# Expert 0's rows by one-hot matmuls from token rows split in SBUF, and its tables spread over its products

## The chip, the cores and the metric

The kernel runs on one core of one Trainium2 chip. The metric is the device time of one execution in microseconds (us). The kernel before takes 1868.66, the median of three runs (1867.42 to 1868.82). Engine names: PE is TensorE, DVE is VectorE, ACT is ScalarE, POOL is GpSimd, SP is SyncE (here it issues most transfers).

## What is computed

One encoder layer on 1024 tokens of 1024 numbers: windowed attention and multi-scale pooling, gated and mixed, an out-projection with LayerNorm, then a mixture of 32 experts with 4 per token, and a second LayerNorm.

```
mixed = g_attn * a_br + g_pool * p_br
h = layer_norm(DEEPNORM_ALPHA * h + mixed @ w_out, ln1_g, ln1_b)
logits = h @ w_router + b_router
top_vals, top_idx = lax.top_k(logits, 4);  gates = softmax(top_vals)
for each expert e, on the rows xb that chose it:
    u = xb @ w_mlp1[e] + b_mlp1[e]
    gate = minimum(u[:, :1024], 7);  up = clip(u[:, 1024:], -7, 7)
    y = ((up + 1) * gate * sigmoid(1.702 * gate)) @ w_mlp2[e] + b_mlp2[e]
h = layer_norm(DEEPNORM_ALPHA * h + sum over a token's experts of gates * y, ln2_g, ln2_b)
```

## The kernel before

All large products run as three matmuls of 16-bit parts: an f32 operand is split into hi (f16) and lo (bf16, what hi leaves), and hi*hi, lo*hi and hi*lo are summed in PSUM. Every engine executes its instructions in the order in which the program writes them; nothing reorders them, so an instruction that waits holds up all that stands behind it on its engine. Tiles are handed over by semaphores.

**The dense stage** (`dense`) ends with the out-projection: a loop over 8 tiles t of 128 tokens. The mixed branches lie transposed and split in `mth` and `mtl` (written in `branch`, L555 and L556). One iteration makes two column halves c: 24 matmuls into a PSUM tile `pb`, L602 adds the residual into `z`, and LayerNorm takes statistics (L57); after both halves `rstd` and `apply` (L74, L75 for each half) finish z, the new h of the tile. Between these steps the loop weaves the router of the tile before (`Router`, called `hooks`): 8 transposes of z (L673), ACT's `hh` (L681) and DVE's `hl` (L682) make the split transposed rows, 24 small matmuls the logits (L696 to L698), `topk`, `pos_mm` and `place` give each token its place in its experts' lists and write the one-hot rows `oh` of expert 0 (L974), `gates` the softmax (ACT's `e`, L748), `tables` a transposed table `P4T` (L768). `hooks.step(t - 1)` at the top of iterations 1 to 6 prefetches one half of expert 0's weights: ACT's `wh` (L943) and DVE's `wl` (L948), 128x2048 each. z is written in f32 to `hD` in DRAM.

**The expert stage** (`experts`, `main`) takes the 32 experts r in order of load, with capacities from 176 down to 109 rows. An expert is 6 products: four column blocks of W1, (1, r, 0) to (1, r, 3), and two of W2, of 96 matmuls each (L1088 to L1090); the list `seq` interleaves the W2 products of expert r - 1 with the W1 products of r. Product i prepares the weights of product i + 2 (3 buffers): `wh` half 0, `wl` half 0, `wh` half 1, and `wl` half 1 at its end. Around the products hang tables of steps: `start`, `mid` (after the first of a product's groups, 48 matmuls), `end`.

For a later expert the chain is: `onehot(r)` on DVE (8 instructions, from the ranks table `spr`), `slot_mm(r)` (16 matmuls, L1003, from `cols`), `gather(r)` (DVE's `ig`, then POOL's indirect DMA of f32 rows of `hD`, L1019), `x_tr` (8 f32 transposes per tile, L1053), `x_hi` (ACT's `xh`, L1064) and `x_lo` (DVE's `xl`, L1069). For expert 0 this runs at the start of `main`, before product 0. `ranks` sorts the experts by load (`key` to `eb`), reads the order and the biases (`eid`, `b1r`, `b2r`), makes `spr` and `cols` from `P4T` (L834, L836), and an overflow table (30 small DVE instructions, L841 to L872); all of it behind `cum4` stands in the middle of product 0, and gather(1) at its end. After the last W1 product of an expert ACT makes `ah` (L1137) and DVE `al` (L1148), which the W2 products read; in DVE's order a `wl` stands ahead of `al`.

## Time and profile before

| | us |
|---|---|
| median of 3 runs | 1868.66 (1867.42 to 1868.82) |
| profiled execution, its own time | 1867.19 |
| its span in the trace | 1865.3 |
| dense stage up to the last logits | 572.6 |
| product 0 begins | 595.3 |
| product 3 begins | 631.6 |
| TensorE / DVE / ACT busy, share of the span | 94% / 83% / 65% |
| granted TensorE clock, mean (1 is 2.4 GHz) | 0.979 |

The span runs from the first to the last instruction that the trace holds. A share of busy time is a mean over stages with different limits, so the stages have to be read apart. Idle time of an engine that is not the bottleneck costs nothing.

### The profile page before, as it was taken

What the parts mean: (1) busy time and instruction counts of PE and PEld (TensorE: products, weight loads), DVE (VectorE), ACT (ScalarE), POOL (GpSimd) and SP (SyncE); (2) the same over time, 40 slices, a digit from 0 to 9 for tenths busy, and PEclk for the clock granted to TensorE, in tenths of its full rate; (3) what the DMA queues carried; (4) which work ended last, traced back from release to release, by engine and by line L of the source; (5) the groups of instructions that cost most, each with busy time, mean ns of one, the idle gap of its engine ahead of it and who ended that gap; (6) DMA issues with size and microseconds to landing.
All of it is one profiled execution on the core that took longest, in us unless ns stands there. A gap on an engine that the chain in (4) does not pass through costs nothing.

```text
span 1865.3 us, 53770 instructions
## 1 busy us (share of the span) xinstructions
PE 1759.6 (94%) x23150; PEld 1496.6 (80%) x23150; DVE 1555.0 (83%) x2248; ACT 1221.7 (65%) x1679; POOL 555.6 (30%) x586
## 2 busy tenths in 40 slices
PE   7998999999896999999999999999999999999980
PEld 6455554444444999999999999999999999999980
DVE  4587863234696999999999999999999999999985
ACT  4455632223121588888778888888888888888873
POOL 1336420000012523354333343234332432342111
PEclk9999999999997999999999999999999999999995
DMA  5100032112554699999999999999999999999965
GB/s 181 52 24 24 24 100 67 46 46 100 208 209 180 215 330 363 367 359 352 338 349 358 359 356 367 358 373 363 370 366 376 375 362 373 374 372 365 366 231 200
DMA packets 245955, 494.20 MB, mean 265 GB/s; under 512 B 10982, under 2 KB 32870, under 8 KB 245712
## 3 DMA queue, kind: packets, MB, share of 16 engines
q1 hardware_dynamic: 234432, 453.03, 67.3%
q0 software_dynamic: 10992, 36.62, 8.0%
q8 instruction: 184, 3.01, 0.7%
q10 hardware_dynamic: 288, 1.05, 0.1%
q14 instruction: 59, 0.48, 0.1%
HBM read 458.34 MB, written 32.33 MB: 263 GB/s over the span
## 4 chain that ended last, share of the span: by engine, by line
PE 76%; DVE 13%; ACT 4%; issue 3%; DMA 2%; POOL 0%; SPq 0%; POOLq 0%; DVEq 0%; ACTq 0%
PE mm L1088 18%; PE mm L1090 18%; PE mm L1089 18%; PE mm L108 4%; PE mm L107 4%; PE mm L109 4%; DVE wl L948 3%; PE tr L1157 2%; PE tr L1053 2%; PE pb L109 2%; PE pb L107 2%; PE pb L108 2%; ACT wh L943 1%; DVE s L344 1%; DVE ms L346 1%
## 5 line engine op out<-in xcount | busy, mean ns | idle before, releaser
L948 DVE SCALAR_TENSOR_TENSOR wl<-raw,wh 128x2048 bf16<-128x2048 f32 x384 | 874.0, 2285 | 23.4 <-ACT wh L943 22.9
L1090 PE MATMUL mm<-xh,wl 128*128 128x123 f16 (+30 forms) x4096 | 743.9, 223 | 1.9 <-DVE wl L948 1.8
L1088 PE MATMUL mm<-xh,wh 128*128 128x123 f16 (+30 forms) x4096 | 744.2, 223 | 0.6 <-ACT xh L1064 0.6
L1089 PE MATMUL mm<-xl,wh 128*128 128x123 bf16 (+30 forms) x4096 | 743.9, 223 | 0.3 <-DVE nv L745 0.3
L943 ACT ACTIVATE wh<-raw 128x2048 f16<-128x2048 f32 x384 | 725.9, 1910 | 11.4 <-PE mm L1089 8.8
L1090 PEld LDWEIGHTS <-wl 128*128 128x128 bf16 x6144 | 598.1, 97 | 5.7 <-DVE wl L948 2.7
L1089 PEld LDWEIGHTS <-wh 128*128 128x128 f16 x6144 | 598.7, 97 | 3.6 <-issue 2.8
L1088 PEld LDWEIGHTS <-wh 128*128 128x128 f16 x6144 | 596.6, 97 | 0.9
L1088 PE MATMUL mm<-ah,wh 128*128 128x123 f16 (+30 forms) x2048 | 372.6, 223 | 2.1 <-ACT ah L1137 2.1
L1089 PE MATMUL mm<-al,wh 128*128 128x123 bf16 (+30 forms) x2048 | 372.4, 223 | 1.9 <-DVE al L1148 1.9
L1090 PE MATMUL mm<-ah,wl 128*128 128x123 f16 (+30 forms) x2048 | 372.4, 223 | 0.0
L1019 POOL DMA_INDIRECT x<-hD,ig x51 | 71.8, 1408 | 563.9 <-DVE st L1008 298.9
L1169 POOL DMA_INDIRECT accD<-y,is x51 | 109.0, 2137 | 226.8 <-ACT yT L1112 96.4
L107 PE MATMUL mm<-xth,wh 128*128 128x512 f16 x400 | 151.7, 379 | 1.2 <-DVE ypl L102 1.1
L109 PE MATMUL mm<-xth,wl 128*128 128x512 f16 x400 | 151.6, 379 | 0.0
L108 PE MATMUL mm<-xtl,wh 128*128 128x512 bf16 x400 | 151.6, 379 | 0.0
L1165 ACT ACTIVATE y<-tr,gt 128x512 f32<-128x512 f32 (+11 forms) x102 | 65.3, 682 | 59.9 <-PE tr L1157 31.1
L109 PEld LDWEIGHTS <-wl 128*128 128x128 bf16 x528 | 51.7, 98 | 62.3
L108 PEld LDWEIGHTS <-wh 128*128 128x128 f16 x528 | 51.7, 98 | 56.8 <-issue 1.3
L1132 ACT ACTIVATE th<-pre 128x492 f32<-128x492 f32 (+30 forms) x64 | 42.3, 661 | 81.9 <-DVE pre L1120 81.9
L107 PEld LDWEIGHTS <-wh 128*128 128x128 f16 x528 | 51.7, 98 | 55.0 <-DVE kk L211 0.2
L161 DVE SCALAR_TENSOR_TENSOR wl<-raw,wh 128x768 bf16<-128x768 f32 (+1 forms) x30 | 24.3, 865 | 81.9 <-ACT wh L157 81.7
(305 smaller groups left out, 2545.5 us busy)
## 6 DMA issues: line engine op xcount, KB each, us to landing
raw<-in_w_mlp_dram SPq DMA_DIRECT2D x384, 1024.0 KB, 12.0
raw<-in_w_in_dram SPq DMA_DIRECT2D x13, 1024.0 KB, 5.2
...
```

What stands on the lines that cost most here:

```text
L107: nc.tensor.matmul(ps, wh(k), xh(k), start=first and i == 0, stop=False)
L108: nc.tensor.matmul(ps, wh(k), xl(k), start=False, stop=False)
L109: nc.tensor.matmul(ps, wl(k), xh(k), start=False, stop=last and i == n - 1)
L943: nc.scalar.activation(WT[i][0][:, a:b], RAW[i, h], AF.Copy, scale=WS)
L948: nc.vector.scalar_tensor_tensor(lo[:, a:b], RAW[i, h], WS, hi[:, a:b], op0=OP.mult, op1=OP.subtract)
L1019: nc.gpsimd.indirect_dma_start(out=x[:n], out_offset=None, in_=hD, in_offset=IO(ap=ig[:n, c], axis=0))
L1088: nc.tensor.matmul(ps[:, j], wh[:, k, fs], h[:, k, :Cr], start=k == 0, stop=False)
L1089: nc.tensor.matmul(ps[:, j], wh[:, k, fs], l[:, k, :Cr], start=False, stop=False)
L1090: nc.tensor.matmul(ps[:, j], wl[:, k, fs], h[:, k, :Cr], start=False, stop=k == KT - 1)
L1132: nc.scalar.activation(th[:, :, :Cr], v, AF.Tanh, scale=0.5 * 1.702 / WS)
L1165: nc.scalar.activation(E[r]["ys"][j][:n, c * 512:(c + 1) * 512], E[r]["yp"][j][:n].rearrange("p a b -> p (a b)"), AF.Copy, scale=E[r]["gt" ...
L1169: nc.gpsimd.indirect_dma_start(out=accD, out_offset=IO(ap=E[r]["is_"][:n, j:j + 1], axis=0), in_=E[r]["ys"][j][:n], in_offset=None, comput ...
```

## The change

`mth` and `mtl` get a layout by token tile, and once the out-projection has used a tile's part, z of that tile is kept there, split: `row_hi`, two ACT copies behind LayerNorm's halves (L684), and `row_lo`, one DVE subtraction of 128x1024 (L688) behind `hl`. `hD` holds the two 16-bit parts of a row side by side instead of f32. Expert 0's x is not gathered: 128 matmuls of 128x176 (`x0_mm`) multiply the rows by the one-hot rows, as far as rows and one-hots are there, and `x0_out` splits the result. Of `ranks`, the order of the experts and the biases now stand in the middle of product 0, the overflow table at its end, `spr` and `cols` in the middle of product 1, slots of expert 0 and `onehot(1)` at the end of product 1, gather(1) in the middle of product 2, its transposes in the middle of product 3. Later experts transpose the 16-bit parts: 16 transposes per tile, and a copy each on ACT and DVE. In the last three products `ah` and `al` stand ahead of the next weights' split.

```diff
-    mth = mp.tile([P, KT, S], F16, name="mth")
-    mtl = mp.tile([P, KT, S], BF16, name="mtl")
+    mth = mp.tile([P, NT, KT, P], F16, name="mth")
+    mtl = mp.tile([P, NT, KT, P], BF16, name="mtl")
...
-                mm3(ps, lambda k: mth[:, k, tk], lambda k: mtl[:, k, tk],
+                mm3(ps, lambda k: mth[:, t, k], lambda k: mtl[:, t, k],
...
-        hooks.pos_mm(t - 1) if t == NT - 1 else None
+        if t == NT - 1:
+            hooks.x0_mm(range(3), range(6))
+            hooks.pos_mm(t - 1)
+            hooks.x0_mm(range(3, 4), range(6))
         for h in range(2):
             ln.apply(z, g1, b1, z, slice(h * 512, (h + 1) * 512))
+            hooks.row_hi(t, h)
             if t == NT - 1:
                 hooks.tr_mm(t, h)
+                hooks.x0_mm(range(4 + h, 5 + h), range(6))
         hooks.write(t, z)
     hooks.place(NT - 2)
     for h in range(2):
         hooks.tr_out(NT - 1, h)
+    hooks.row_lo(NT - 1)
     hooks.logits(NT - 1)
     hooks.topk(NT - 1)
+    hooks.x0_mm(range(4), range(6, KT))
     hooks.pos_mm(NT - 1)
     hooks.place(NT - 1)
+    hooks.gates(NT - 2)
+    hooks.x0_mm(range(4, 7), range(6, KT))
+    hooks.x0_mm(range(6, 7), range(6))
+    hooks.x0_mm(range(7, 8), range(KT))
+    hooks.x0_out()
...
-        nc = self.nc
-        q = nc.scalar if t == NT - 1 else nc.sync
-        q.dma_start(self.hD[t * P:(t + 1) * P, :], z)
+        q = self.nc.scalar if t == NT - 1 else self.nc.sync
         q.dma_start(self.accD[t * P:(t + 1) * P, :], z)
+
+    def row_hi(self, t, h):
+
+        s = slice(h * 4, h * 4 + 4)
+        z = self.z[t][:, h * 512:(h + 1) * 512].rearrange("p (k q) -> p k q", q=P)
+        self.nc.scalar.activation(self.rows[0][:, t, s], z, AF.Copy)
+
+    def row_lo(self, t):
+        nc, (hi, lo) = self.nc, self.rows
+        nc.vector.tensor_sub(lo[:, t], self.z[t].rearrange("p (k q) -> p k q", q=P), hi[:, t])
+        tk = slice(t * P, (t + 1) * P)
+        nc.sync.dma_start(self.hD[tk, :D], hi[:, t].rearrange("p k q -> p (k q)"))
+        nc.sync.dma_start(self.hD[tk, D:], lo[:, t].bitcast(F16).rearrange("p k q -> p (k q)"))
+
+    def x0_mm(self, tiles, ks):
+
+        nc, c = self.nc, self.moe.c0
+        for k2 in range(ks[0] // 2, (ks[-1] + 2) // 2):
+            if k2 not in self.px:
+                ps = self.pb.tile([P, 512], F32, name="pb") if k2 < 3 else self.pt.tile([P, 4, P], F32, name="tp")
+                self.px[k2] = (ps if k2 < 3 else ps.rearrange("p a b -> p (a b)"))[:, :2 * c].rearrange("p (k c) -> p k c", c=c)
+            for k in (2 * k2, 2 * k2 + 1):
+                for t in tiles:
+                    for j in range(2):
+                        nc.tensor.matmul(self.px[k2][:, k % 2], self.rows[j][:, t, k], self.moe.oh0(t),
+                                         start=t == 0 and j == 0 and k % 2 == 0, stop=t == NT - 1 and j == 1 and k % 2 == 1,
+                                         skip_group_check=True)
+
+    def x0_out(self):
+        for k2 in range(4):
+            self.moe.x0_put(k2, self.px.pop(k2))
...
+        self.row_lo(t)
...
+    def x0_put(k2, ps):
+        s = slice(2 * k2, 2 * k2 + 2)
+        nc.scalar.activation(E[0]["xh"][:, s, :caps[0]], ps, AF.Copy)
+        nc.vector.tensor_sub(E[0]["xl"][:, s, :caps[0]], ps, E[0]["xh"][:, s, :caps[0]])
+
+    def oh0(t):
+        return E[0]["oh"][:, t, :caps[0]]
...
         def gather(r):
-                x = wk1.tile([P, D], F32, name=f"x{i}")
+                x = wk1.tile([P, 2 * D], F16, name=f"x{i}")
                 nc.gpsimd.indirect_dma_start(out=x[:n], out_offset=None, in_=hD, in_offset=IO(ap=ig[:n, c], axis=0))
                 xs.append(x)
-            rows(r, 0, 5 if r else 2)
+            E[r].update(xs=xs, xh=None)
+            targets(r)
...
+            i, s0, n, lo = part
+            dt, ident = ((F16, C["ident16"]), (BF16, C["identb"]))[lo]
+            tp = pt.tile([P, KT, n + n % 2], dt, name="tr")[:, :, :n]
+            for k in range(KT):
+                row = E[r]["xs"][i][:n, lo * D + k * P:lo * D + (k + 1) * P]
+                nc.tensor.transpose(tp[:, k], row.bitcast(BF16) if lo else row, ident[:n, :n])
...
-        slot_mm(0, 0, 2)
-        gather(0)
+        router.gates(NT - 1)
         rctx = ExitStack()
         rsb = rctx.enter_context(tc.tile_pool(name="r_sb", bufs=1, reuse_waits="tile"))
         rk = ranks(tc, C, R, rsb, lambda shape, dt: pm.tile(shape, dt, name="mm"))
         next(rk)
-        refill()
-        for part in xparts(0):
-            x_tr(0, part)
-            x_hi(0, part)
-            x_lo(0, part)
-        router.gates(NT - 2)
-        router.gates(NT - 1)
-
-        def tables():
+
+        def order():
             next(rk)
-            slot_mm(0, 2, 5)
-            rows(0, 2, 5)
-            gates(0)
-            onehot(1)
-            for _ in rk:
-                pass
-
-        def first_rows():
-            slot_mm(1)
-            gather(1)
+            refill()
+
+        def late():
+            next(rk)
             rctx.close()
             LATE["b"] = ctx.enter_context(tc.tile_pool(name="e_lb", bufs=2, reuse_waits="tile"))
             LATE["a"] = ctx.enter_context(tc.tile_pool(name="e_la", bufs=1, reuse_waits="tile"))
@@ -1208,20 +1251,32 @@
             for y in LATE["y"][0] + LATE["y"][1]:
                 nc.gpsimd.memset(y, 0.0)
 
-        at(mid, 0, tables)
-        at(end, 0, first_rows)
+        def slots0():
+            slot_mm(0)
+            targets(0)
+            onehot(1)
+
+        at(mid, 0, order)
+        at(end, 0, late)
+        at(mid, 1, next, rk)
+        at(end, 1, slots0)
+        at(mid, 2, slot_mm, 1)
+        at(mid, 2, gather, 1)
         for r in range(1, NR):
             b = first[r]
             if r > 1:
-                at(start, max(b - 9, 0), onehot, r)
-                at(end, max(b - 8, 0), slot_mm, r)
-                at(start, max(b - 7, 1), gather, r)
+                at(start, max(b - 9, 3), onehot, r)
+                at(end, max(b - 8, 3), slot_mm, r)
+                at(start, max(b - 7, 4), gather, r)
             parts = xparts(r)
             for j, part in enumerate(parts):
-                s_ = max(b - 1 - len(parts) + j, 1)
-                at(end, s_, x_tr, r, part)
-                at(x_evac, s_ + 1, x_hi, r, part)
-                at(x_evac, s_ + 1, x_lo, r, part)
+                if r == 1:
+                    at(mid, 3, x_tr, r, part)
+                    at(end, 3, x_out, r, part)
+                else:
+                    s_ = b - 1 - len(parts) + j
+                    at(end, s_, x_tr, r, part)
+                    at(x_evac, s_ + 1, x_out, r, part)
...
+            product = 0 < i <= NS and seq[i - 1][0] == 1
+            if product and i >= NS - 3:
+                post_a(i - 1)
+                post_p(i - 1)
+                product = False
             if split:
                 w_hi(n, 0)
-            if 0 < i <= NS and seq[i - 1][0] == 1:
+            if product:
                 post_a(i - 1)
             if split:
                 w_lo(n, 0)
                 refill()
                 w_hi(n, 1)
-            if 0 < i <= NS and seq[i - 1][0] == 1:
+            if product:
                 post_p(i - 1)
```

ACT in the out-projection loop, before: one iteration with its neighbours (`e` belongs to the gates, `hh` to the router's split rows).

```order
286 L943 ACTIVATE wh<-raw 128x2048
287 L748 ACTIVATE e_5337,den<-vm,nv 128x4
288 L681 ACTIVATE hh<-tp 128x512 x2
289 L768 ACTIVATE P4T<-tp 128x128
290 L943 ACTIVATE wh<-raw 128x2048
291 L748 ACTIVATE e_5496,den<-vm,nv 128x4
```

And now:

```order
288 L811 ACTIVATE P4T<-tp 128x128
289 L684 ACTIVATE mth<-z 128x512 x2
290 L989 ACTIVATE wh<-raw 128x2048
291 L791 ACTIVATE e_5357,den<-vm,nv 128x4
292 L723 ACTIVATE hh<-tp 128x512 x2
293 L811 ACTIVATE P4T<-tp 128x128
294 L684 ACTIVATE mth<-z 128x512 x2
295 L989 ACTIVATE wh<-raw 128x2048
```

The two copies `mth<-z` (they read the finished z) have come in directly ahead of `wh`, which stood behind `P4T`.

DVE at the end of one iteration and the start of the next, before:

```order
571 L74 SCALAR_TENSOR_TENSOR z<-z,ln_mv_4986,g_3409 128x512
572 L75 SCALAR_TENSOR_TENSOR z<-z,ln_r_4987,b_3410 128x512
573 L74 SCALAR_TENSOR_TENSOR z<-z,ln_mv_4986,g_3409 128x512
574 L75 SCALAR_TENSOR_TENSOR z<-z,ln_r_4987,b_3410 128x512
575 L948 SCALAR_TENSOR_TENSOR wl<-raw,wh 128x2048
576 L602 SCALAR_TENSOR_TENSOR z<-pb,xt_4847 128x512
577 L57 BN_STATS ln_st_5141<-z 128x6
```

and in the middle of it, before and now:

```order
555 L753 TENSOR_TENSOR eq<-eq,e_5024 128x128
556 L755 TENSOR_REDUCE G<-eq 128x32
557 L682 TENSOR_TENSOR hl<-tp,hh 128x512 x2
558 L602 SCALAR_TENSOR_TENSOR z<-pb,xt_4775 128x512
559 L57 BN_STATS ln_st_4985<-z 128x6
```

```order
557 L796 TENSOR_TENSOR eq<-eq,e_5036 128x128
558 L798 TENSOR_REDUCE G<-eq 128x32
559 L724 TENSOR_TENSOR hl<-tp,hh 128x512 x2
560 L688 TENSOR_TENSOR mtl<-z,mth 128x1024
561 L603 SCALAR_TENSOR_TENSOR z<-pb,xt_4782 128x512
562 L57 BN_STATS ln_st_4997<-z 128x6
```

`mtl<-z,mth` has come in behind `hl`; the piece around `wl`, from `L74` to `ln_st`, stands as before, so `wl` is still the next instruction behind the last `L75`.

DVE at the end of the ranks' work and the start of the later experts', before (`tabs` is the last of the overflow table, `ig` and `st` are expert 1's, `pre` and `th` the activation):

```order
802 L872 COPY tabs<-tab 128x128
803 L1107 TENSOR_TENSOR pre<-mm,b1r 128x2x176
804 L1017 CAST ig<-sl 128x1
805 L1017 CAST ig<-sl 10x1
806 L1008 COPY st<-sl 128x5
807 L1008 COPY st<-sl 10x5
808 L1038 SCALAR_TENSOR_TENSOR st<-st 128x1
809 L1039 SCALAR_TENSOR_TENSOR st<-st 128x1
810 L1038 SCALAR_TENSOR_TENSOR st<-st 10x1
811 L1039 SCALAR_TENSOR_TENSOR st<-st 10x1
812 L1107 TENSOR_TENSOR pre<-mm,b1r 128x2x176
813 L1120 TENSOR_SCALAR pre<-pre 128x4x176
```

And now, the piece that ends with expert 1's `ig` (`st` in the first rows is expert 0's, `oh` expert 1's one-hot):

```order
807 L1088 COPY st<-sl 128x5
808 L1088 COPY st<-sl 48x5
809 L1102 SCALAR_TENSOR_TENSOR st<-st 128x1
810 L1103 SCALAR_TENSOR_TENSOR st<-st 128x1
811 L1102 SCALAR_TENSOR_TENSOR st<-st 48x1
812 L1103 SCALAR_TENSOR_TENSOR st<-st 48x1
813 L1063 TENSOR_SCALAR oh<-iotaC,spr 128x138 x8
814 L1180 TENSOR_SCALAR pre<-pre 128x4x176
815 L1181 SCALAR_TENSOR_TENSOR pre<-pre,th 128x4x176
816 L994 SCALAR_TENSOR_TENSOR wl<-raw,wh 128x2048
817 L1205 TENSOR_TENSOR al<-pre,ah 128x4x176
818 L1077 CAST ig<-sl 128x1
```

`ig` stood behind `tabs` and one `pre`, ahead of product 3's `wl`; now both halves of product 3's `wl`, the tables `spr` and `cols`, the one-hots and the first half of product 4's `wl` stand ahead of it.

## Rows read from the trace of the kernel before

**Rows 1.** The page's first part: busy time of each engine, its share of the span and its instructions.

```profile
PE 1759.6 (94%) x23150; PEld 1496.6 (80%) x23150; DVE 1555.0 (83%) x2248; ACT 1221.7 (65%) x1679; POOL 555.6 (30%) x586
```

**Rows 2.** The table by stretches: the stretch and its length, busy time (and number of instructions) of PE, PEld, DVE, ACT and POOL, then TensorE's granted clock, the DMA share and GB/s; a stretch of the out-projection loop, one of the passage to the experts, one of the products.

```profile
500.00:520.00 20.00, 17.47 (x131) 9.28 (x129) 18.32 (x45) 4.52 (x9) 3.96 (x16) 1.00 0.68 239
580.00:600.00 20.00, 13.25 (x168) 11.61 (x167) 10.88 (x43) 3.55 (x9) 5.61 (x20) 0.50 0.67 239
660.00:760.00 100.00, 100.00 (x1620) 99.06 (x1618) 95.00 (x123) 83.30 (x100) 32.78 (x31) 1.00 1.00 349
```

**Rows 3.** DVE's timeline over one iteration of the out-projection loop: start, duration, engine, line, operation, tiles and shapes, and in brackets the idle time before it with its releaser.

```profile
512.48 2.28 DVE L948 SCALAR_TENSOR_TENSOR wl<-raw,wh 128x2048 bf16<-128x2048 f32 x1
...
517.12 0.16 DVE L751 RECIPROCAL den<-den 128x1 f32<-128x1 f32 x1 [0.46 <-ACT e L748]
...
525.45 0.75 DVE L75 SCALAR_TENSOR_TENSOR z<-z,ln_r,b 128x512 f32<-128x512 f32 x1
526.12 2.28 DVE L948 SCALAR_TENSOR_TENSOR wl<-raw,wh 128x2048 bf16<-128x2048 f32 x1
```

**Rows 4.** ACT's timeline in the same iteration.

```profile
520.05 0.28 ACT L768 ACTIVATE P4T<-tp 128x128 f16<-128x128 f16 x1 [1.99 <-PE tp L767]
520.23 1.90 ACT L943 ACTIVATE wh<-raw 128x2048 f16<-128x2048 f32 x1
```

**Rows 5.** The waits from 500 to 570: the waiting engine and operation, its releaser, us in total, times, longest.

```profile
PE mm L698 <- DVE hl L682: 5.5, 5, 1.1
```

**Rows 6.** Groups of instructions by line and shape: count, busy us and mean ns of one, then the idle time before them. ACT's copy into `mth` in the branches, DVE's `hl` in the loop, and an operation of 128x1024 in f32 in the last LayerNorm.

```profile
L555 ACT ACTIVATE mth<-t 128x512 f16<-128x512 f32 x3 | 1.9, 629 | 9.5 <-DVE t L554 9.5
L682 DVE TENSOR_TENSOR hl<-tp,hh 128x512 bf16<-128x512 f32 x10 | 6.4, 678 | 0.0
L1508 DVE SCALAR_TENSOR_TENSOR a<-a,sums,g 128x1024 f32<-128x1024 f32 x8 | 10.0, 1278 | 0.0
```

**Rows 7.** DVE's timeline behind the loop, as far as expert 1's `ig`.

```profile
572.24 0.69 DVE L602 SCALAR_TENSOR_TENSOR z<-pb,xt 128x512 f32<-128x512 f32 x1 [0.40 <-PE pb L109]
...
582.48 0.19 DVE L706 SCALAR_TENSOR_TENSOR lg<-mm,br 128x32 f32<-128x32 f32 x1 [0.55 <-PE mm L698]
...
613.76 0.20 DVE L1017 CAST ig<-sl 128x1 int32<-128x1 f32 x2
```

**Rows 8.** TensorE's timeline behind the loop, as far as product 3.

```profile
575.70 0.18 PE L726 MATMUL mm<-mask,upper 128*128 128x32 f16 x1 [2.84 <-DVE mask L718]
577.75 1.08 PE L673 MATMUL tp<-identf,z 128*128 128x128 f32 x4 [1.85 <-DVE z L75]
...
591.73 2.98 PE L1053 MATMUL tr<-identf,x 128*128 128x128 f32 x16 [0.82 <-DMA x<-hD,ig]
595.30 0.31 PE L1088 MATMUL mm<-xh,wh 128*128 128x176 f16 x1 [0.58 <-ACT xh L1064]
...
604.33 0.24 PE L1003 MATMUL sl<-cols,oh 128*128 128x3 f16 x4 [1.31 <-DVE cols L836]
605.61 0.53 PE L1003 MATMUL sl<-cols,oh 128*128 128x3 f16 x12 [1.04 <-DVE cols L836]
...
622.12 1.10 PE L1053 MATMUL tr<-identf,x 128*128 128x128 f32 x8 [2.74 <-DMA x<-hD,ig]
623.05 0.24 PE L1088 MATMUL mm<-xh,wh 128*128 128x176 f16 x1
...
631.58 0.25 PE L1088 MATMUL mm<-xh,wh 128*128 128x176 f16 x1
631.67 0.24 PE L1089 MATMUL mm<-xl,wh 128*128 128x176 bf16 x1
...
631.90 0.24 PE L1089 MATMUL mm<-xl,wh 128*128 128x176 bf16 x1
```

**Rows 9.** DVE alone in two stretches: busy time (and instructions), granted clock of TensorE, DMA share, GB/s.

```profile
585.80:591.40 5.60, 3.21 (x17) 0.50 0.42 129
602.60:622.30 19.70, 18.15 (x74) 0.91 0.35 85
```

**Rows 10.** POOL's timeline: the first gather of expert 1.

```profile
614.19 1.04 POOL L1019 DMA_INDIRECT x<-hD,ig  x1 [6.88 <-DVE st L1008]
```

**Rows 11.** All of TensorE's waits from 660 to 1780, columns as in rows 5.

```profile
PE mm L1090 <- DVE wl L948: 0.8, 2, 0.4
```

**Rows 12.** Groups of DVE's instructions from 660 to 1780, columns as in rows 6: the subtraction that makes `xl` of a full tile.

```profile
L1069 DVE TENSOR_TENSOR xl<-tr,xh 128x512 bf16<-128x512 f32 x36 | 24.5, 681 | 0.0
```

**Rows 13.** TensorE's timeline ahead of the last product.

```profile
1806.31 0.21 PE L1088 MATMUL mm<-ah,wh 128*128 128x109 f16 x1 [2.15 <-ACT ah L1137]
1808.37 0.25 PE L1089 MATMUL mm<-al,wh 128*128 128x109 bf16 x1 [1.85 <-DVE al L1148]
```

**Rows 14.** DVE's timeline in the same place.

```profile
1805.51 2.28 DVE L948 SCALAR_TENSOR_TENSOR wl<-raw,wh 128x2048 bf16<-128x2048 f32 x1
1807.71 0.61 DVE L1148 TENSOR_TENSOR al<-pre,ah 128x436 bf16<-128x436 f32 x1
```

**Rows 15.** TensorE's timeline early in the program.

```profile
32.64 1.65 PE L198 MATMUL tp<-identf,xt 128*128 128x128 f32 x8 [2.51 <-DVE xtl L102]
```

**Rows 16.** TensorE alone in two stretches behind that row: busy time (and instructions), granted clock, DMA share, GB/s.

```profile
33.00:37.00 4.00, 4.00 (x33) 0.57 0.76 255
40.00:45.00 5.00, 4.93 (x59) 1.00 0.00 0
```

More of the change, by code (lines that the diff above doesn't have):

```diff
@@ L583, in dense @@
     load_x2(1)
-    hooks.begin(ctx, pt, pm)
+    hooks.begin(ctx, pt, pm, pb, mth, mtl)
     for t in range(NT):
-        tk = slice(t * P, (t + 1) * P)
         load_x2(t + 2)
@@ L641, in __init__, with begin @@
         self.z, self.hT, self.st, self.lp, self.pp, self.sp, self.tp = {}, {}, {}, {}, {}, {}, {}
-    def begin(self, ctx, pt, pm):
+    def begin(self, ctx, pt, pm, pb, mth, mtl):
         nc, tc = self.nc, self.tc
-        self.pt, self.pm = pt, pm
+        self.pt, self.pm, self.pb, self.rows, self.px = pt, pm, pb, (mth, mtl), {}
         self.rs = self.moe.open_weights()
@@ L822, in ranks @@
     nc.vector.tensor_scalar(R["b2r"], pb[:, :8], WS * WS, None, op0=OP.mult)
-    yield
-    for t in range(NT - TL, NT):
-        tp = ptile([P, P], F16)
-        nc.tensor.transpose(tp, R["P4"][:, t].rearrange("p a e -> p (a e)"), C["ident16"])
-        nc.scalar.activation(R["P4T"][:, t], tp, AF.Copy)
-    cols = R["cols"]
-    for h in range(2):
-        pq = ptile([P, 512], F32).rearrange("p (t a e) -> p t a e", t=4, a=4)
-        for t in range(4):
-            nc.tensor.matmul(pq[:, t], R["P4T"][:, h * 4 + t], bd.rearrange("p a e -> p (a e)"), start=True, stop=True)
-        nc.vector.tensor_copy(R["spr"][:, :, h * 4:h * 4 + 4], pq[:, :, 0].rearrange("p t r -> p r t"))
-        for j in range(3):
-            nc.vector.tensor_copy(cols[:, :, h * 4:h * 4 + 4, 2 + j], pq[:, :, 1 + j].rearrange("p t r -> p r t"))
     yield
@@ L874, in ranks @@
     nc.sync.dma_start(R["ovS"], tabs)
+    yield
+    for t in range(NT - TL, NT):
+        tp = ptile([P, P], F16)
+        nc.tensor.transpose(tp, R["P4"][:, t].rearrange("p a e -> p (a e)"), C["ident16"])
+        nc.scalar.activation(R["P4T"][:, t], tp, AF.Copy)
+    cols = R["cols"]
+    for h in range(2):
+        pq = ptile([P, 512], F32).rearrange("p (t a e) -> p t a e", t=4, a=4)
+        for t in range(4):
+            nc.tensor.matmul(pq[:, t], R["P4T"][:, h * 4 + t], bd.rearrange("p a e -> p (a e)"), start=True, stop=True)
+        nc.vector.tensor_copy(R["spr"][:, :, h * 4:h * 4 + 4], pq[:, :, 0].rearrange("p t r -> p r t"))
+        for j in range(3):
+            nc.vector.tensor_copy(cols[:, :, h * 4:h * 4 + 4, 2 + j], pq[:, :, 1 + j].rearrange("p t r -> p r t"))
     nc.sync.dma_start(R["sprD"], R["spr"])
     nc.sync.dma_start(R["colD"], cols)
+    yield
 def spread(n):
@@ L965, in oh_tile, with x_pool, x_alloc @@
         return oh
+    def x_pool(b):
+        PL["x", b] = ctx.enter_context(tc.tile_pool(name=f"e_x{b}", bufs=1, side="right", reuse_waits="tile"))
+    def x_alloc(r):
+        cm = max(caps[r % 2::2])
+        E[r]["xh"] = PL["x", r % 2].tile([P, KT, cm], F16, name="xh")
+        E[r]["xl"] = PL["x", r % 2].tile([P, KT, cm], BF16, name="xl")
+    def x0_put(k2, ps):
[4 more added lines that the diff above has]
+        return E[0]["oh"][:, t, :caps[0]]
     def prefetch(t):
@@ L1002, in slot_mm @@
                 for t in range(NT):
-                    nc.tensor.matmul(pl[:n, i, c0:c1], E[r]["oh"][:, t, s0:s0 + n], cols[:, r, t, c0:c1],
+                    nc.tensor.matmul(pl[:n, i, :5], E[r]["oh"][:, t, s0:s0 + n], cols[:, r, t],
                                      start=t == 0, stop=t == NT - 1)
-        def rows(r, c0=0, c1=5):
-            for i, (s0, n) in enumerate(E[r]["rows"]):
-                nc.vector.tensor_copy(E[r]["st"][:n, i, c0:c1], E[r]["pl"][:n, i, c0:c1])
         def gather(r):
-            E[r]["st"] = st = sm.tile([P, 2, 8], F32, name="st")
             ig = sm.tile([P, 2], I32, name="ig")
-            is_ = sm.tile([P, 2], I32, name="is")
             xs = []
@@ L1319, in leftover @@
         x = sb.tile([P, D], F32, name="ox")
-        nc.gpsimd.indirect_dma_start(out=x, out_offset=None, in_=hD, in_offset=IO(ap=ig[:, 0:1], axis=0))
+        xr = sb.tile([P, 2 * D], F16, name="oxr")
+        nc.gpsimd.indirect_dma_start(out=xr, out_offset=None, in_=hD, in_offset=IO(ap=ig[:, 0:1], axis=0))
+        nc.vector.tensor_add(x, xr[:, :D], xr[:, D:].bitcast(BF16))
         xt = sb.tile([P, KT, P], F32, name="oxt")
@@ L1370, in encoder @@
         make_identity(nc, identf)
-        hD = dr.tile([S, D], F32, name="hD")
+        hD = dr.tile([S, 2 * D], F16, name="hD")
         accD = dr.tile([S + NTRASH, D], F32, name="accD")
```

59 lines of the change are left out of this document (30 added, 29 removed).

## The prediction

> **What bounds the kernel now.** The page first: TensorE is busy 94% of the span, but DVE 83% as well [rows 1]. A share of the whole hides the stages, so the table by stretches comes next [rows 2]. In the out-projection loop (500 to 520) it is DVE that is full, 18.3 of 20 us, while ACT works 4.5 and TensorE waits a little; from 580 to 600 nobody is full, and TensorE runs at half its clock; in the expert products (660 to 760) TensorE has no idle time at all. The same microsecond on DVE therefore costs a microsecond in the loop, and nothing that one can see in the products.
>
> DVE's own timeline shows the loop's period: `wl` begins at 512.48 and again at 526.12, so an iteration takes 13.64 us [rows 3]. Between the two, every instruction begins as its forerunner ends, except `den`, which waits 0.46 for ACT's `e`. DVE's order is therefore the loop's clock. ACT's timeline says why `wl` waits for nothing though it reads ACT's `wh`: that `wh` ran at 520.23, right behind `P4T`, 4 us before DVE came to it at 526.12 [rows 4]. TensorE waits once per iteration, 1.1 us, for `hl` [rows 5].
>
> **The change part by part.** The sum is made against the profiled execution's 1867.19 us, which is 1.5 below the median of the runs shown; I add that at the end.
>
> *1. ACT's `mth<-z` ahead of `wh`, six iterations.* The change issues two ACT copies of z into `mth` after the LayerNorm's halves, and in ACT's order they stand ahead of the `wh` of the next iteration. The second needs DVE's last `L75`. So `wh`, which ran early, can't begin until `L75` has ended (526.12 by the next start), and DVE's very next instruction is the `wl` that needs it. DVE then waits for one copy of 128x512 and one `wh`: 0.63 and 1.90 by their own rows [rows 4, 6], 2.5 us. Behind the waiting `wl` on DVE stands the whole next iteration: z, the router, `hl`, LayerNorm. There is no cover: DVE is the bound. Weights are prefetched in iterations 1 to 6 only, so 6 x 2.5 = **15.0**.
>
> *2. DVE's `mtl<-z,mth`, 128x1024, once per tile.* No such operation is in the trace. The nearest are `hl`, 0.68 for 128x512 (two would be 1.36), and L1508, 1.28 for 128x1024 in f32 [rows 6]. One instruction saves the second one's start, so I take 1.2, with 1.0 and 1.4 as ends. In those six iterations: 6 x 1.2 = **7.2** (6.0 to 8.4). In the last iteration, which has no `wl`, DVE waits 0.40 for TensorE at z [rows 7], so 0.8 of the seventh is felt; it belongs to item 3. The loop alone costs 22.2.
>
> *3. From the last logits to expert 1.* Times here are those of before, with the loop's 22.2 taken off.
> Today this stretch is a chain of short waits: TensorE stands 2.84 and 1.85 us at 575.70 and 577.75, then 0.82 for the gathered x at 591.73, and product 0 begins at 595.30; in it TensorE waits 1.31 and 1.04 for `cols`, and 2.74 at 622.12 for the gather of expert 1; product 3 begins at 631.58, and so product 4 at 631.58 + 96 x 0.076 = 638.9 [rows 8].
> New: 128 one-hot matmuls of 176 columns. Product 0's own have that width and are 0.076 apart at the full clock (631.67 to 631.90: three steps in 0.23): 9.7 us, of which 72 fall into the waits of 2.84 and 1.85 and around them. The seventh tile's `lg` comes later by 0.8 and by `mtl<-z,mth` of tile 7, 1.2, less what its wait of 0.55 for TensorE covers [rows 7]: about 1.6, at 584.1. From there DVE does top-k, `oh`, the gates of tile 6, four `xl`, the gates of tile 7 and only then `cum4`, which the first table matmul needs: 1.9 + 0.5 + 2.0 + 2.0 + 2.0, at 592.5. Product 0 begins near 592.8, **2.5 earlier** than today, since the gather and its transposes (591.73) are gone from the way.
> What was spread is still DVE's. Its work from `cum4` to today's `wl` is 3.2 us busy in 585.8 to 591.4 and 18.2 in 602.6 to 622.3 [rows 9]; in the new order the `ig` of expert 1 stands behind all of it but 2 us of one-hots, and behind one more `wl`, `pre` and `al`, 4.5: some 24. I add 7 of waits: 2 for TensorE in the ranks as today, and 5 for `P4T`, which ACT reaches only behind two `wh`, and for `wh`. So `ig` comes at about 623.5 instead of 613.76 [rows 7]. A gather takes 7.9 from its start on POOL at 614.19 to TensorE at 622.12 [rows 8, 10]. The transposes of expert 1 then begin at 631.5 in the middle of product 3, take 1.5, and 48 matmuls remain, 3.6: product 4 at 637, **1 to 2 earlier**. I take -1; ends -7 (the clock stays up and DVE's waits vanish) and +5 (the gather of expert 2 and the next `wl` come late too, DVE having no slack).
> The cover that is gone: the waits for `cols` and the first gather are replaced by one for `P4T` and one for the second gather.
>
> *4. Later experts.* Per tile 16 transposes of 16 bits for 8 of f32. Eight f32 ones of a full tile take 0.93 (622.12 to 623.05); a 16-bit one of 128 columns I bound by the 0.076 of a 176-column matmul from above: 1.2; and by 128/176 of that from below: 0.88. DVE's two subtractions of 0.68 become one copy of 128x1024, ACT's two copies one [rows 12]. TensorE waits 0.8 us in all of 660 to 1780 [rows 11], so a gain on DVE is worth nothing there. 0; ends -2 and +8 (31 full tiles by -0.05 and +0.27).
>
> *5. The last product.* TensorE stands 1.85 us at 1808.37 for `al`, which on DVE stands behind a `wl` of 2.28 from 1805.51 [rows 13, 14]. The change puts `al` first: it could begin when `ah` is there, which TensorE had at 1806.31, and take its 0.61; I take 1.5 off the wait, and 0.5 of half clock behind it: **-2** (-1.2 to -3.2).
>
> *6. At nothing:* the new layout of `mth` in the branches (the same instructions), the two hD transfers for one (same bytes, on SP's queue, read only some 30 us later), one more constant.
>
> Sum: 1867.2 + 15.0 + 7.2 - 1 - 2 = 1886.4; with 1.5 to the median **1888**.
>
> **The rivals.**
> *A. The boundary gives it all back (not slower).* From 572.64 to 638.85 are 66.2 us, with some 37.5 of TensorE's work at full clock (384 matmuls of four products at 0.076 are 29.2; transposes, logits and tables some 8.4); the other 28.7 is wait and half clock. The 128 new matmuls need 9.7, which leaves 19. If TensorE never waits for `cum4`, `P4T` or the gather, the time is 1867.2 + 22.2 - 19 - 3 + 1.5 = 1869. It decides from the point at which `ig` of expert 1 comes by 615 instead of 623.5. For it: the idle time is there, and the spread tables do leave TensorE more to run under them. Against: DVE's 24 us don't shrink. Chance 0.07; with 5 us more, faster.
> *B. `wl` doesn't wait* (ACT could take `wh` first, or a buffer lets DVE pass): then only part 2: 1867.2 + 7.2 - 3 + 1.5 = 1873. Against it stands ACT's order. Chance 0.06.
> *C. TensorE's clock falls in the loop.* Its wait per iteration grows from 1.1 to some 4.7 us. At 32.64 the trace has a wait of 2.51 [rows 15], and behind it the granted clock of 33 to 37 is 0.57 of 2.4 GHz, that is 1.2 GHz for most of it [rows 16]. Half clock for some 3.5 us costs TensorE 1.8 an iteration, less than the 3.7 that DVE's longer period gives it, so I cost it at nothing. If it lasted the whole iteration, TensorE's 12 us of work would be 24, beyond DVE's 17.3: 6 x 6.7 = 40 more, 1928. Against: TensorE worked on from there, and from 40 to 45 the clock is 1.00 again. Chance 0.05. The Trainium skill ("TensorE: Matmul & The Clock Gate", Why this matters for your kernels) speaks against this change here: it asks for no long idle gaps between bursts of matmuls, or the clock goes back to its lower level. By that rule the loop would come under C; the row at 32.64 agrees that the clock falls.
>
> **How the numbers follow.** The forecast's own case has 0.82: 1888, with its ends 1888 - 6 - 2.5 and + 6 + 4 not reached at once: 1880 to 1896. The low end goes down to B and stops short of A (1873); the high one, 1898, takes in a bad boundary with slower transposes and leaves C out. What a measurement of this kernel can tell from no change is about 0.2%, 3.7 us: faster means under 1865, which only the better part of A gives, 0.04; same, A's rest and a good B, 0.06; slower 0.90.
>
> **What would show it.** Right: in the loop `wl` every 17.3 us, with a wait of 2.5 <-ACT `wh`, and ACT's `wh` directly behind the second `mth<-z`; one `mtl<-z,mth` of 1.2 per tile; product 0 about 20 us later than 595.30; in the products waits for `P4T` and for x of expert 1; the wait for `al` nearly gone. Wrong: a loop of 14.8 us (B), clock rows of 0.5 to 0.7 in the loop with DVE waiting for TensorE (C), product 4 at 642 or earlier (A).

## The result, and the profile after

The changed kernel takes 1887.68 us (median of 4 runs, 1884.53 to 1888.01) against 1868.04 for the kernel before (4 runs, 1867.39 to 1868.82), a ratio of 1.0104 with a 95% interval of 1.0092 to 1.0116. It is slower by 19.6 us, 1.0%; 1888 was forecast. The sum came out, but not every term did, as the marks below show.

First the place that carries the forecast, DVE's timeline in the loop after the change (it answers to [rows 3]):

```profile
539.83 2.29 DVE L994 SCALAR_TENSOR_TENSOR wl<-raw,wh 128x2048 bf16<-128x2048 f32 x1 [2.50 <-ACT wh L989]
...
545.55 1.28 DVE L724 TENSOR_TENSOR hl<-tp,hh 128x512 bf16<-128x512 f32 x2
546.75 1.22 DVE L688 TENSOR_TENSOR mtl<-z,mth 128x1024 bf16<-128x1024 f32 x1
...
553.95 0.75 DVE L75 SCALAR_TENSOR_TENSOR z<-z,ln_r,b 128x512 f32<-128x512 f32 x1
557.20 2.29 DVE L994 SCALAR_TENSOR_TENSOR wl<-raw,wh 128x2048 bf16<-128x2048 f32 x1 [2.50 <-ACT wh L989]
```

`wl` now begins every 17.37 us instead of 13.64, with 2.50 of idle time in brackets that were not there, and `mtl<-z,mth` is the new row. ACT's timeline of the same iteration shows what the 2.50 consist of (compare [rows 4]):

```profile
553.28 0.63 ACT L684 ACTIVATE mth<-z 128x512 f16<-128x512 f32 x1 [5.53 <-DVE z L75]
554.74 0.63 ACT L684 ACTIVATE mth<-z 128x512 f16<-128x512 f32 x1 [0.82 <-DVE z L75]
555.27 1.89 ACT L989 ACTIVATE wh<-raw 128x2048 f16<-128x2048 f32 x1
```

ACT sits idle 5.53 us in front of the first copy, with the `wh` behind it ready to run. An engine that is idle most of the time still delayed the busiest one, because of what stood first in its order.

TensorE in the loop, two waits of one iteration, and the table of one stretch (columns as in [rows 2]):

```profile
579.72 0.19 PE L739 MATMUL mm<-wrh,hh 128*128 128x32 f16 x1 [2.30 <-ACT hh L723]
...
581.03 0.21 PE L741 MATMUL mm<-wrh,hl 128*128 128x32 f16 x1 [1.09 <-DVE hl L724]
```

```profile
540.00:560.00 20.00, 16.76 (x101) 8.43 (x99) 16.46 (x34) 4.70 (x8) 3.33 (x9) 0.91 0.46 155
```

Its one wait of 1.1 [rows 5] has become 2.3 and 1.1, and the granted clock 0.91 instead of 1.00: part of every iteration runs at 1.2 GHz. DVE, whose busy share fell from 18.3 of 20 us to 16.5 (and to 14.0 in the 20 us ahead of these, which hold two of its waits), is nevertheless what sets the period: its 17.37 are the 13.64 of before, 2.50 and 1.22, to 0.01.

Then the passage to the experts, TensorE (it answers to [rows 8]) and DVE (to [rows 7]):

```profile
612.09 0.18 PE L826 MATMUL mm<-cumE,ones 128*128 128x32 f16 x1 [1.49 <-DVE nv L788]
613.87 0.18 PE L827 MATMUL mm<-ones,cum 128*128 128x1 f16 x1 [1.60 <-DVE cum L824]
...
631.74 0.61 PE L916 MATMUL mm<-bd,P4T 128*128 128x128 f16 x8 [2.47 <-ACT P4T L911]
...
661.00 0.23 PE L1145 MATMUL mm<-xh,wh 128*128 128x138 f16 x1
```

```profile
619.95 0.22 DVE L850 COPY eidf<-mm 128x64 f32<-128x64 f32 x1 [4.22 <-PE mm L848]
...
632.16 0.29 DVE L917 COPY spr<-mm 128x128 f32<-128x128 f32 x1 [0.31 <-PE mm L916]
...
641.56 2.28 DVE L994 SCALAR_TENSOR_TENSOR wl<-raw,wh 128x2048 bf16<-128x2048 f32 x1
643.76 0.88 DVE L1205 TENSOR_TENSOR al<-pre,ah 128x704 bf16<-128x704 f32 x1
644.56 0.20 DVE L1077 CAST ig<-sl 128x1 int32<-128x1 f32 x2
```

Product 0 begins at 613.90, right behind `cum4`; `ig` of expert 1 comes at 644.56, behind the row of `wl` and `al` as the order had it; product 4 begins at 661.00. In between TensorE's clock falls behind its waits. Three stretches of 48 product matmuls and the few rows at their edges, TensorE alone (columns as in [rows 9], with TensorE for DVE); ahead of them stand waits of 1.49 and 1.60, of 2.47, and of 1.30 and 1.68:

```profile
613.90:619.28 5.38, 5.38 (x49) 0.68 0.03 11
632.18:637.47 5.29, 5.29 (x52) 0.68 0.64 95
654.28:660.44 6.16, 6.16 (x51) 0.57 0.82 292
```

At the full clock 48 of these take 3.65 (638.04 to 641.69). So in this execution waits of 2.5 to 3.1 us are paid once as waits and again, 1.6 to 2.5, as slow matmuls behind them. Not every kernel of this study pays the second time, as the runs on the passage show.

Ahead of the last product, TensorE (compare [rows 13]):

```profile
1827.64 0.21 PE L1145 MATMUL mm<-ah,wh 128*128 128x109 f16 x1 [1.25 <-ACT ah L1194]
...
1828.29 0.21 PE L1146 MATMUL mm<-al,wh 128*128 128x109 bf16 x1 [0.45 <-DVE al L1205]
```

And the marks of the two profiled executions, read from TensorE's timelines, in us. The marks are starts, but for the out-projection, where the end of the last matmul is given, and the end of the span. (The 572.6 that the table of before gives for the last logits is the end of tile 6's, the last in the loop; those of tile 7 end at 582.4.)

| mark | before | after | later by |
|---|---|---|---|
| last matmul of the out-projection | 572.20 | 594.64 | 22.44 |
| product 0 | 595.30 | 613.90 | 18.60 |
| product 4 | 638.87 | 661.00 | 22.13 |
| product 6 | 650.39 | 674.45 | 24.06 |
| product 12 | 691.72 | 715.89 | 24.17 |
| product 186 | 1781.30 | 1805.19 | 23.89 |
| last product matmul | 1818.99 | 1837.89 | 18.90 |
| end of the span | 1865.34 | 1885.80 | 20.46 |

The last column shows where time went and where it came back: 22.4 in the loop; 3.8 won up to product 0 and lost again up to product 4, 1.9 more lost up to product 6; nothing in 180 products; 5.0 won at the end; 1.6 lost in the tail.

A caution for all such marks: six kernels of this study with the same code up to the loop begin their first prefetched `wl` anywhere between 488.4 and 491.0, so a mark of one execution is good to some 2.6 us. Differences within one execution are steadier: the periods of the loop repeat to 0.1 from the second `wl` on, and from the end of the out-projection to product 4 three kernels with the same passage take 66.4, 67.5 and 67.5.

### The profile page after: what moved, and what is told of

It reads as the page before. It is cut to its first block, busy times and chain, and to the rows that moved or that the text cites. A ratio compares the mean times of both kernels' runs of the same rounds, so it can differ in the third digit from the quotient of the medians.

```text
span 1885.8 us, 54663 instructions
## 1 busy us (share of the span) xinstructions
PE 1772.2 (94%) x23638; PEld 1500.3 (80%) x23638; DVE 1544.6 (82%) x2223; ACT 1230.1 (65%) x1665; POOL 547.4 (29%) x584
## 5 line engine op out<-in xcount | busy, mean ns | idle before, releaser
L1226 POOL DMA_INDIRECT accD<-y,is x51 | 109.3, 2143 | 237.0 <-ACT yT L1169 67.5
L1161 ACT ACTIVATE pre<-mm,b1r 128x176 f32<-128x176 f32 (+30 forms) x256 | 76.8, 369 | 27.8 <-PE mm L1147 27.7
```

The lines of the kernel that those rows point to most:

```text
L1161: nc.scalar.activation(o[:, j], ps[:, j], AF.Identity, scale=0.5 / WS, bias=b1r[:, f0 + g + j, r:r + 1])
L1226: nc.gpsimd.indirect_dma_start(out=accD, out_offset=IO(ap=E[r]["is_"][:n, j:j + 1], axis=0), in_=E[r]["ys"][j][:n], in_offset=None, comput ...
```

## The experiments

The theory was that DVE's order is the loop's clock, with two prices, 2.5 for the wait and 1.2 for the subtraction. The rival: the loop got longer because TensorE waits and runs at the lower clock, and DVE's wait only shows that.

**`wh` ahead of the copies.**

```diff
     def prefetch(t):
         if 0 <= t < 6:
-            w_hi(t // 2, t % 2)
             w_lo(t // 2, t % 2)
             refill(1)
+    def prefetch_hi(t):
+        if t < 6:
+            w_hi(t // 2, t % 2)
...
+        hooks.moe.prefetch_hi(t)
         for h in range(2):
             ln.apply(z, g1, b1, z, slice(h * 512, (h + 1) * 512))
             hooks.row_hi(t, h)
```

> The changed kernel with one thing moved: ACT's wh of the next iteration is issued ahead of the two copies mth<-z of this one (wl stays in its place). Theory (DVE's order is the loop's clock, and 2.5 us of an iteration are its wait for wh behind mth<-z): the period falls from 17.37 to 14.85 us, no wait of wl for wh is left in the loop, 6 x 2.5 = 15.0 less, about 1872.7. Rival (the loop got longer because TensorE runs part of each iteration at 1.2 GHz, granted clock 0.91 there, and waits for hh; DVE's wait only shows that): the wait moves on to another instruction and the time falls by under 5, 1883 or more.

Measured: 1869.89 (1865.96 to 1874.27, 11 runs), ratio to the kernel before 1.001, interval 0.9999 to 1.0021. DVE's timeline in the loop:

```profile
514.53 2.28 DVE L995 SCALAR_TENSOR_TENSOR wl<-raw,wh 128x2048 bf16<-128x2048 f32 x1
519.17 0.16 DVE L795 RECIPROCAL den<-den 128x1 f32<-128x1 f32 x1 [0.46 <-ACT e L792]
521.45 1.23 DVE L689 TENSOR_TENSOR mtl<-z,mth 128x1024 bf16<-128x1024 f32 x1
529.32 2.28 DVE L995 SCALAR_TENSOR_TENSOR wl<-raw,wh 128x2048 bf16<-128x2048 f32 x1
```

No bracket is left at `wl`, and the period is 14.79, against a forecast of 14.85. The out-projection ends 7.2 later than before instead of 22.4. The order of these instructions on an engine that is mostly idle was worth 15.2 us in the loop, of the 19.6 by which the kernel had become slower; the rival falls. The clock says so too: of two iterations that follow each other here one has a granted clock of 0.88 and the next 1.00, and both take 14.79. The median is 17.8 under the changed kernel's, 2.8 more than forecast, with runs spread over 8 us; the profiled execution, 1873.86, is the second slowest of the eleven, so its trace does not show where the 2.8 come from.

**The copies alone, in the kernel before.**

```diff
         for h in range(2):
             ln.apply(z, g1, b1, z, slice(h * 512, (h + 1) * 512))
+            hooks.row_hi(t, h)
...
+    def row_hi(self, t, h):
+        z = self.z[t][:, h * 512:(h + 1) * 512].rearrange("p (k q) -> p k q", q=P)
+        self.nc.scalar.activation(self.mth[:, h * 4:h * 4 + 4, t * P:(t + 1) * P], z, AF.Copy)
```

> The kernel before with ACT's two copies mth<-z per tile and nothing else of the change; nobody reads what they write. Theory: wl waits 2.5 us for wh in six iterations, 15.0 more than before, about 1883. Rival (ACT has room, 4.5 of 20 us busy, and the copies disappear in it): 1868, no change.

Measured: 1885.65 (1881.85 to 1887.57, 5 runs), ratio 1.0093 (1.0075 to 1.0111). Eight tiles with two small copies that nobody reads make the kernel 0.9% slower. In its loop DVE's `wl` shows the same wait:

```profile
536.38 2.29 DVE L954 SCALAR_TENSOR_TENSOR wl<-raw,wh 128x2048 bf16<-128x2048 f32 x1 [2.50 <-ACT wh L949]
...
552.60 2.29 DVE L954 SCALAR_TENSOR_TENSOR wl<-raw,wh 128x2048 bf16<-128x2048 f32 x1 [2.50 <-ACT wh L949]
```

In two iterations TensorE's granted clock differs, 0.79 and 1.00, and the period does not (columns as in [rows 2]):

```profile
520.16:536.38 16.22, 12.36 (x70) 5.57 (x69) 12.68 (x32) 4.70 (x8) 2.48 (x9) 0.79 0.48 161
536.38:552.60 16.22, 15.00 (x99) 7.78 (x98) 12.68 (x32) 4.70 (x8) 2.48 (x9) 1.00 0.48 163
```

So the lower clock is not what lengthens the loop. The out-projection ends 15.4 later than before, and the products keep 14.5 of it. The median is 18 above the kernel before, 3 more than that; the profiled execution took 1882.86, at the low end of the five, so the trace does not show where the others spent the rest.

**The subtraction twice.**

```diff
-        nc.vector.tensor_sub(lo[:, t], self.z[t].rearrange("p (k q) -> p k q", q=P), hi[:, t])
+        for _ in range(2):
+            nc.vector.tensor_sub(lo[:, t], self.z[t].rearrange("p (k q) -> p k q", q=P), hi[:, t])
```

> The changed kernel with the subtraction mtl<-z,mth issued twice per tile, the second writing the same numbers again. Theory (DVE is full in the loop): six iterations longer by 1.22 each, 7.3, and up to 2.0 more for tiles 6 and 7: 1895 to 1897. Rival (TensorE's waits and clock set the period): under 3 more, below 1891.

Measured: 1895.64 (1893.44 to 1896.13), 8.0 above the changed kernel; the period is 18.63, that is 17.37 and 1.26. DVE has no slack in the loop.

**The subtraction on POOL,** with `wh` first.

```diff
+        hooks.row_sub(t)
         hooks.write(t, z)
...
+    def row_sub(self, t):
+        hi, lo = self.rows
+        self.nc.gpsimd.tensor_sub(lo[:, t], self.z[t].rearrange("p (k q) -> p k q", q=P), hi[:, t])
+
     def row_lo(self, t):
         nc, (hi, lo) = self.nc, self.rows
-        nc.vector.tensor_sub(lo[:, t], self.z[t].rearrange("p (k q) -> p k q", q=P), hi[:, t])
```

> The kernel of e1_wh_first with the subtraction mtl<-z,mth on POOL, issued right behind the second mth<-z of its tile, instead of on DVE behind hl. Theory (the rest of the loop's growth is DVE's 1.22 per tile): the loop's period falls to some 13.6 us, as before the change, and the end of the out-projection comes 7.2 earlier than in e1_wh_first: about 1862, under the kernel before by some 5. Rival (POOL, which also makes ln_r and the gates' parts, is late with them behind a subtraction that it takes over 2 us for, and DVE waits for ln_r): the period stays at 14.6 or more, 1868 or more.

Measured: 1865.06 (1862.45 to 1868.80, 11 runs), ratio 0.9977 (0.9968 to 0.9985): below the kernel before, by 3.7 instead of 5 or more. The period is 13.98, not 13.64. The missing 0.34 is not POOL being late with `ln_r`, but an instruction of DVE's own. The groups by shape in the loop, DVE's one-hot of the changed kernel, and below it the same and POOL's subtraction of this one:

```profile
L1038 DVE TENSOR_SCALAR oh<-iotaC,sp 128x176 f16<-128x176 f16 x4 | 1.2, 299 | 0.1
```

```profile
L1046 DVE TENSOR_SCALAR oh<-iotaC,sp 128x176 f16<-128x176 f16 x6 | 4.5, 750 | 0.2
L690 POOL TENSOR_TENSOR mtl<-z,mth 128x1024 bf16<-128x1024 f32 x6 | 19.3, 3218 | 30.5 <-ACT mth L686 30.5
```

The means mix two cases. In each of the five iterations POOL subtracts for 3.4 us (DVE needs 1.22), and DVE's one-hot takes 0.60 instead of 0.30; in the sixth, behind the last `wl`, POOL takes 2.13 and the one-hot 1.48. All six one-hots end 0.05 to 0.06 behind the end of POOL's subtraction, and the two later ones, beside which POOL does not subtract, take 0.27 as they did before. With `cum` behind it, 0.20 instead of 0.16, this is the 0.34.

**The last products.** Once taken out of the change, once put alone into the kernel before:

```diff
-            if product and i >= NS - 3:
-                post_a(i - 1)
-                post_p(i - 1)
-                product = False
```

> The changed kernel without its reordering in the last products: ah and al stand behind the next weights' split again, as before. By the prediction's term the time rises by 2.0, to 1889.7. By the two traces, which put the last matmul 5.0 us earlier relative to the product that begins 37 us ahead of it, it rises by 5.0, to 1892.7. A third reading, that what is won there is partly lost in the tail behind the last matmul (1.6 us longer in the profile): by 3.4, to 1891.1.

Measured: 1887.89 (1886.95 to 1889.44), no different from the changed kernel: none of the three expected times came, and the time shows no gain from the reordering inside the change.

> The kernel before with the reordering in the last three products alone (ah and al ahead of the next weights' split). By the prediction's term 2.0 less than before, 1865.5. If the 5.0 by which the last matmul came earlier in the trace of the change were all its own: 1862.5. Rival (the tail behind the last matmul takes it back): 1867.

Measured: 1866.79 (1864.09 to 1869.41, 12 runs), ratio 0.999 (0.9981 to 0.9999): 2.0 less than before, as the prediction's term, though the interval goes from 0.2 to 3.6 less and so leaves room for the rival as well. In the traces, from product 186 to the last product matmul the four kernels take 37.7 (before), 35.3 (reordering alone), 32.7 (the change) and 34.1 (the change without it). By these pairs the reordering is 1.4 to 2.4 of the 5.0; the 1.4 is not firm, since the other kernels that have the reordering take 32.7 to 34.4. The rest comes with the other parts: in the kernel before, 83 of the matmuls behind the wait take 5.57, in the change without the reordering 4.01. The clock fell behind these waits in the one and not in the other, though they are alike (2.15 and 1.85 against 1.82 and 1.85); whether it falls there is not settled by what I ran.

**The passage.** Two readings stood against each other: TensorE's waits set it, or DVE's order.

```diff
+    for t in range(NT - TL, NT):
+        tp = ptile([P, P], F16)
+        nc.tensor.transpose(tp, R["P4"][:, t].rearrange("p a e -> p (a e)"), C["ident16"])
+        nc.scalar.activation(R["P4T"][:, t], tp, AF.Copy)
     yield
...
-    for t in range(NT - TL, NT):
-        tp = ptile([P, P], F16)
-        nc.tensor.transpose(tp, R["P4"][:, t].rearrange("p a e -> p (a e)"), C["ident16"])
-        nc.scalar.activation(R["P4T"][:, t], tp, AF.Copy)
     cols = R["cols"]
```

The added lines run in the middle of product 0, the removed ones ran in the middle of product 1.

> The changed kernel with the last three P4T transposes and ACT's copies in the middle of product 0, ahead of product 3's wh, instead of in the middle of product 1. If TensorE's own waits set the passage, its wait of 2.5 for P4T and the half clock behind it (48 matmuls in 5.29 instead of 3.65) go: product 4 some 4 earlier, about 1883.5. If DVE's order sets it (spr and cols stand behind wl and th, and DVE waits 0.31 there for TensorE), TensorE waits longer at the transposes of expert 1 instead: under 1 earlier, about 1887.

Measured: 1888.79 (1886.82 to 1889.96). The wait of 2.47 is gone and 48 matmuls behind it take 3.64, yet product 4 is 65.9 behind the end of the out-projection instead of 66.4: the transposes of expert 1 now wait 2.77 and 1.45. `ig` stands 49.5 behind that end instead of 49.9. The kernels with this passage unchanged (the change, the one with `wh` first, and the one without the reordering at the end) spread over 66.4 to 67.5 and 49.9 to 51.1, so at most 1.6 of the 4 expected by the first reading came. So DVE's order decided here.

```diff
+    def fill(out, n):
+        for _ in range(n):
+            nc.tensor.matmul(out, C["ident16"], C["ident16"], start=True, stop=True)
+    fill(pc[:, 256:384], 25)
     nc.tensor.matmul(pc[:, :NE], C["ones"], R["cum"], start=True, stop=True)
+    fill(pc[:, 256:384], 28)
...
+        fill(pq[:, 0], 40 * (1 - h))
```

> The changed kernel with 93 matmuls of 128x128 into unread PSUM columns put into TensorE's three waits of the passage: 25 and 28 around the first table matmul, 40 ahead of the matmuls that wait for P4T. They do no part of the computation. If the half clock behind those waits sets the passage (first half of product 0 in 5.38 instead of 3.65, of product 1 in 5.29 instead of 3.65, and DVE waits 4.2 for product 0's middle): the granted clock stays at 1.00, product 4 some 3 earlier, about 1884.5. If DVE's order alone sets it: under 1 earlier, about 1887; if the fillers are too long, up to 1 later.

Measured: 1890.55 (1889.64 to 1891.17). This one told little, through the edit: the first 25 and the 40 wrote PSUM tiles that were themselves waited for, so they ran behind the waits and not in them, and DVE's wait for `spr` grew from 0.31 to 2.54. The next puts them right, 27 between the two table matmuls and 42 into a tile of their own ahead of the third transpose:

```diff
     nc.tensor.matmul(pc[:, :NE], C["ones"], R["cum"], start=True, stop=True)
+    fill(pc[:, 256:384], 27)
...
+    spare = ptile([P, 512], F32)
+    fill(spare[:, :P], 1)
     for t in range(NT - TL, NT):
+        fill(spare[:, :P], 42 if t == NT - 1 else 0)
```

> As e8_fill_waits, with the fillers where they run inside the waits and not behind them: 27 matmuls of 128x128 between the first two table matmuls, 42 between the second and the third transpose for P4T, into PSUM columns nobody reads; they do no part of the computation. If the half clock behind the waits is part of the passage's path: the first half of product 0 takes 3.7 instead of 5.4 and that of product 1 3.65 instead of 5.3, DVE's wait of 4.2 in product 0 shrinks by 1.7 and expert 1's ig comes that much earlier; product 4 some 2 to 3 earlier behind the end of the out-projection (now 66.4 us), about 1885. If DVE's own work sets it: 66 or more, no change within 1 us.

Measured: 1885.15 (1883.46 to 1887.55), 2.5 under the changed kernel; the two intervals of the ratio to the kernel before (1.0076 to 1.0107, and 1.0092 to 1.0116) overlap, so the time alone does not settle it. Its trace does, in the first two of the three stretches and on DVE:

```profile
616.50:620.25 3.75, 3.75 (x50) 1.00 0.08 27
633.40:637.00 3.60, 3.60 (x51) 1.00 0.83 86
653.98:659.50 5.52, 5.52 (x68) 0.75 0.82 292
```

```profile
620.91 0.22 DVE L855 COPY eidf<-mm 128x64 f32<-128x64 f32 x1 [2.57 <-PE mm L853]
...
633.29 0.29 DVE L925 COPY spr<-mm 128x128 f32<-128x128 f32 x1 [0.47 <-PE mm L924]
...
644.65 0.20 DVE L1085 CAST ig<-sl 128x1 int32<-128x1 f32 x2
```

The clock stays at 1.00, DVE's wait of 4.22 becomes 2.57, `ig` comes 47.4 behind the out-projection's end instead of 49.9, and product 4 begins 62.3 behind it instead of 66.4.

Two kernels above show the same without any filler. The one with the subtraction twice and the one with it on POOL have the same waits of 1.49 and 1.60 ahead of product 0, and its first half ran at clock 1.00 all the same; below each stretch stands DVE's wait for it:

```profile
625.01:628.67 3.66, 3.66 (x49) 1.00 0.02 7
629.41 0.23 DVE L851 COPY eidf<-mm 128x64 f32<-128x64 f32 x1 [2.57 <-PE mm L849]
...
594.20:597.85 3.65, 3.65 (x49) 1.00 0.02 6
598.60 0.23 DVE L855 COPY eidf<-mm 128x64 f32<-128x64 f32 x1 [2.56 <-PE mm L853]
```

From product 0 to `ig` these two take 27.9 and 28.8, and the kernel with fillers 28.1; the three kernels with the passage unchanged, where these 48 matmuls take 5.3 to 6.4, need 30.7 to 31.8. So the passage is DVE's order, and one link of that order waits for TensorE at half clock. What these runs do not show is that the fillers keep the clock up: without them it fell behind these waits in four kernels and not in two, and why is open.

**Both together.** The kernel with `wh` first, the subtraction on POOL, and these fillers:

> The kernel of e4_row_lo_pool with the fillers of e9_fill_inside. If e9's gain is there and adds up: 2 to 3 below e4_row_lo_pool, about 1862.5. If the passage is DVE's: as e4_row_lo_pool, about 1865.

Measured: 1863.14 (1860.56 to 1865.70, 8 runs), ratio 0.9974 (0.9963 to 0.9984). It has the lowest median of the kernels run here, 4.8 under the kernel before. Against the one with POOL alone nothing is shown: the medians differ by 1.9, but the ratios, each to the kernel before run beside it, are 0.9974 and 0.9977. The traces agree: product 4 stands 63.2 behind the out-projection's end here and 62.9 there, where the clock was up in product 0 without fillers.

## Why the prediction was right, point by point

*The wait of `wl` (15.0).* Right in mechanism and size: 2.50 in the trace, 15.2 when taken away, 15.4 when put alone into the kernel before.

*The subtraction (7.2).* Right: 1.22 instead of 1.2; taken off by the run on POOL but for 0.34 an iteration, doubled by the run with two.

*The passage (-1).* The steps were where the order showed them, and most sizes held: product 0 at 591.5 on the scale of before (613.90 less the loop's 22.44) for a forecast of 592.8, `ig` at 622.1 for 623.5. The sum was off. To product 4 it is -0.3, and then 1.9 are lost that I had put only into the upper end: product 6 waits behind the gather of expert 2, which comes late like the first, and behind transposes that now stand right ahead of it. Up to product 6 the term is +1.6 where -1 was said. What I had left out is the clock: I counted the matmuls behind each wait at 0.076, and the trace has 48 of them in 5.3 to 6.2. This is what the Trainium skill ("TensorE: Matmul & The Clock Gate", Why this matters for your kernels) warns of where it asks for no long idle gaps between bursts of matmuls, and I had weighed it for the loop alone. The trace of the change agrees with it in both places (granted clock 0.91 in the loop, 0.57 to 0.68 in the three stretches), but two kernels kept the full clock behind the same waits ahead of product 0. The fall costs nothing in the loop, where TensorE has slack, and 2.5 (by `ig`) to 4 (by product 4) in the passage, where DVE waits for TensorE.

*The later experts (0).* Right: 24.17 at product 12, 23.89 at product 186, with TensorE full in 100 of 100 us from 680 to 780.

*The last product (-2).* Alone the reordering is worth what was said, 2.0, but taken out of the change it makes no difference that the time shows (1887.89 against 1887.68), so inside the change this term did not come as forecast. The last matmul came 5.0 earlier, since two shorter waits for `wl` (0.57 and 0.43) and a fall of the clock also went, which I had not seen as the change's. Against it stands a tail that is longer by 1.6, which I had at nothing: POOL's last scatter starts 2.65 us behind TensorE's last transposes instead of 1.49. All kernels with the rest of the change show 2.65 or more, the kernel before and the two built on it 1.48 or 1.49. That is 1.2 of the 1.6; what POOL does there is in no row, and this stays open.

*The rivals.* A (the boundary gives it all back) failed at its own point: `ig` came at 622 and not by 615. B (no wait at `wl`) did not happen. C happened in part, a granted clock of 0.91 in the loop, and cost nothing there, as the term said: with `wh` first the period came down by 2.58, the wait of 2.50 and 0.08 more, and iterations at different clocks took equally long. TensorE's waits grew to 3.4 us an iteration and not to 4.7, since its own work took 14.0 instead of 12.4.

So the total is better than its parts: 22.2 was forecast for the loop and 22.4 measured, which is no luck, but the errors of the small terms, +2.6 in the passage, -3.0 at the last product and +1.6 in the tail, nearly cancel, and that the sum met the median within 0.3 is luck. The range of 25 us was wide enough for such errors.
